# Delta-rule layer of a decoder trunk: decays on ScalarE, lengths summed on TensorE, masks later, block transfers issued by ScalarE

## The chip, the core and the metric

The kernel runs on one core of a Trainium2 chip. The metric is device time in microseconds (us) of one execution; lower is better. TensorE (PE in the rows, PEld for its weight loads), VectorE (DVE), ScalarE (ACT), GpSimd (POOL) and SyncE (SP) run their own instruction streams in order and wait for each other through semaphores. Transfers (DMAs) are started by an instruction in one of these streams; before the change that stream is SyncE's.

## The reference

A trunk of four layers on 256 positions of width 1024. Layer i mixes tokens by attention (layers 0 and 3), a short convolution (layer 1) or a gated delta rule (layer 2); each layer then has a convolutional feed-forward part (FFN). Only the delta-rule layer, `gdn` in the kernel, is changed:

```python
def gated_deltanet(h, w_in, conv_w, a_log, dt_bias, norm_w, w_o):
    ...
    q = l2norm(q) * (dh ** -0.5)          # 8 heads of 128
    k = l2norm(k)
    beta = jax.nn.sigmoid(b_logit)
    g = -jnp.exp(a_log.astype(f32)) * jax.nn.softplus(a_in + dt_bias.astype(f32))
    ...
    gc = jnp.cumsum(g, axis=-1)
    diff = gc[..., :, None] - gc[..., None, :]
    decay = jnp.where(incl, jnp.exp(jnp.where(incl, diff, 0.0)), 0.0)
    a_mat = jnp.where(strict, jnp.einsum('bhnid,bhnjd->bhnij', k_beta, k) * decay, 0.0)
    t_mat = lax.linalg.triangular_solve(a_mat + eye, ...)   # (a_mat + I)^-1
    u = t_mat @ v_beta
    attn = jnp.where(incl, jnp.einsum('bhnid,bhnjd->bhnij', q, k) * decay, 0.0)
    ...
```

The remaining lines carry a state from chunk to chunk, normalise, gate by `silu(z)` and project back.

## The kernel before, in words

**Products.** All weights come as one stream of 128 x 1024 chunks (`wraw`), loaded by SyncE. ScalarE rounds each chunk to `whi`, VectorE forms the rest `wlo`, several chunks ahead of TensorE. A product adds three matmuls per weight tile, into PSUM banks named `mm`; small matmuls go to four rotating banks named `sm`.

**Order.** TensorE's order is fixed when the program is written. `Weave` keeps a clock: the stream of products (`fill`) advances it, and generator steps such as `lengths`, `systems`, `invert` and `join_half` are put between products when they fall due; a step yields its TensorE time and how long to wait until its next one (the `L_` constants and `LAG`). The other engines' order is made by a scheduler from the data dependences. `after(inst)` binds an instruction to a place behind TensorE's last one, for that scheduler alone.

**The delta rule.** The eight heads form two halves of four, with two chunks of 128 positions, so a half has eight 128 x 128 systems. `decays` forms the decay matrices (`big`), `queries_keys` convolves q and k (`yqk`), `lengths` transposes them and sums their squares, and `systems` forms both score matrices of each system in `aq`: index 1 for keys, index 0 for queries. `invert` inverts the 16 x 16 diagonal blocks: `aq` goes to DRAM (`d<-aq`), comes back with blocks on partitions (`bl<-d`), GpSimd inverts them in 29 small steps (`xb`, `xm`), and the result goes out (`d<-xb`) and back (`xc<-d`). `join16`, `join_half(32)` and `join_half(64)` join blocks into 128 x 128 inverses, in turns between TensorE and the engines that read its results. Then come `solve`, the state, `scores` and `finish` for both chunks, and `output`, which writes `yh`, `yl` (also named `big`). The closing `residual` product consumes them: its first half of contraction (96 matmuls) needs the first half of the heads, named `o0`, its second half needs `o1`.

In `join_half` TensorE makes three groups of small matmuls (`sm<-xt,m`, `sm<-m,xt`, `sm<-xt,m`). The third is released by the copy `big<-sm` on ScalarE that empties the first group's bank:

```python
                    for m in range(NS):
                        PE.matmul(cols(pzt[up], m), lhsT=pm[dn, m, :], rhs=xt(dn, m), start=True, stop=True)
                    S.copy(s.xt[up, :, dn], wide(pzt[up, :NS * n]))
```

Of the kernel before, what the change touches and what calls it, by code (L numbers as in the profile page):

```python
# [15 lines left out]
P = 128  # L16
# [4 lines left out]
H = 8  # L21
# [17 lines left out]
SCALED = 5  # L39
LAG = 1.75  # L40
L_HEAD, L_SOFTMAX, L_TURN, L_MIX, L_READY = 3.5, 9.0, 1.0, 2.5, 0.5
L_QK, L_V, L_LEN, L_SYS, L_BLOCKS, L_JOIN, L_XI, L_PM, L_OUT = 6.0, 6.0, 1.0, 0.5, 6.0, 13.0, 1.0, 2.5, 1.0


PV_MIX = 0
# [10 lines left out]
C_ONE = C_ID + P  # L56
C_BASE = C_ONE + P
C_TRI = C_BASE + 3 * P
C_NEG = C_TRI + P
C_BD = C_NEG + P  # L60
C_LV = C_BD + P
C_UP = C_LV + P
C_EO = C_UP + P
# [4 lines left out]
def constants():  # L68
    i = np.arange(P)
    c = np.zeros((P, C_N), np.float32)  # L70
    c[:, C_ID:C_ID + P] = np.eye(P)
    c[:, C_ONE:C_ONE + P] = 1.0
    dist0 = i[:, None] - i[None, :]
    dist1 = P + i[:, None] - np.arange(2 * P)[None, :]
    base = np.concatenate([dist0, dist1], 1).astype(np.float32)
    c[:, C_BASE:C_BASE + 3 * P] = np.where(base >= 0, base, 1e33)
    c[:, C_TRI:C_TRI + P] = i[:, None] <= i[None, :]
    c[:, C_NEG:C_NEG + P] = np.where(i[None, :] >= i[:, None], 0.0, -1e30)
# [140 lines left out]
def trunk(ctx: ExitStack, tc: tile.TileContext, xT, wstream, pvec, cst, wba, hv, out):  # L219
# [380 lines left out]
    def gdn(gain):  # L600
        nm = Norm()
        NS = 2 * G_H
        with tc.tile_pool(name="gdn", bufs=1) as pool, \
# [12 lines left out]
            dl = pool.tile([P, H], F32, name="dl")  # L616
            eg = pool.tile([P, H], F32, name="eg")
            neg = pool.tile([P, H], F32, name="neg")
            yh, yl = {}, {}

            def big(dt=F32):
# [5 lines left out]
            def gates():  # L627
# [15 lines left out]
                for t in range(2):  # L643
# [19 lines left out]
                PE.matmul(pg[:, 2 * H:3 * H], lhsT=ones, rhs=g[:, 0, :], start=False, stop=True,  # L663
                          skip_group_check=True)
                V.tensor_copy(gc.rearrange("p a b -> p (a b)"), pg[:, :3 * H])
                V.tensor_sub(dl, gc[:, 2, :], gc[:, 0, :])
                S.activation(dl, dl, AF.Exp)
                S.activation(eg, gc[:, 1, :], AF.Exp)
# [6 lines left out]
            class Half:  # L675


                def __init__(self, h0):
                    self.h0, self.y = h0, []

            def decays(s):

                s.dt = big().rearrange("p (a t) i -> p a t i", t=2)
                for a2 in range(0, G_H, 2):
                    pd = bank("sm")
                    for q in range(4):
                        h, t = s.h0 + a2 + q // 2, q % 2
                        PE.matmul(pd[:, q * P:(q + 1) * P], lhsT=g[:, t, h:h + 1].to_broadcast([P, P]),
                                  rhs=tri, start=True, stop=True)
                    for q in range(4):  # L690
                        a, t = a2 + q // 2, q % 2
                        V.scalar_tensor_tensor(s.dt[:, a, t, :], pd[:, q * P:(q + 1) * P],  # L692
                                               gc[:, t, s.h0 + a:s.h0 + a + 1], cs[:, C_NEG:C_NEG + P],
                                               op0=ALU.subtract, op1=ALU.add)
                    yield 0.9, 0
                S.activation(s.dt, s.dt, AF.Exp)
                wv.set(f"d{s.h0}")

            def queries_keys(h, ps):
                yield 0, ("norm",)  # L700
                u = pool.tile([P, 2, T], F32, name="u", bufs=4)
                V.tensor_mul(u, pairs(ps), nm.rb2)
                y = pool.tile([P, 2, T], F32, name="yqk", bufs=H)
# [4 lines left out]
                halves[h // G_H].y.append(y)  # L708
                wv.set(f"q{h}", L_QK)

            def lengths(s):
# [6 lines left out]
                for a in range(G_H):  # L718
                    yield 0, (f"q{s.h0 + a}",)
                    pt = bank("sm")  # L720
                    for i in range(4):
                        q, t = divmod(i, 2)
                        PE.transpose(pt[:, i * P:(i + 1) * P], s.y[a][:, q, t * P:(t + 1) * P], ident)
                    S.copy(s.kt[:, a, :], pt[:, 2 * P:3 * P])
                    for i in range(4):
                        q, t = divmod(i, 2)
                        m = 2 * a + t
                        jk = pool.tile([P, P], F32, name="jk", bufs=1)
                        S.activation(jk, pt[:, i * P:(i + 1) * P], AF.Square, accum_out=sm[:, q, m:m + 1])  # L729
                    yield 0.22, L_LEN  # L730
                yield 0, ("gates",)

                V.tensor_scalar(sj[:, 0, :], sm[:, 0, :], EPS, float(P), op0=ALU.add, op1=ALU.mult)
# [8 lines left out]
                V.tensor_mul(s.kt, s.kt, sw.unsqueeze(2).to_broadcast([P, G_H, P]))  # L742
                wv.set(f"l{s.h0}")

            def systems(s):
# [3 lines left out]
                for a in range(G_H):  # L749
# [6 lines left out]
                    for t in range(2):  # L756
# [2 lines left out]
                            "p (q i) -> p q i", q=2), s.sk[:, m:m + 1],  # L759
                            s.dt[:, a, t, :].unsqueeze(1).to_broadcast([P, 2, P]), op0=ALU.mult, op1=ALU.mult)  # L760
                    yield 0.87, 0.5 * LAG

                nb = P // BLK
                row = (BLK * P + BLK) * nb
                d1 = dram.tile([NS * row], F32, name="d1")
                nc.sync.dma_start(
                    out=d1.rearrange("(m x) -> m x", m=NS)[:, :P * P].rearrange("m (p c) -> p m c", p=P),
                    in_=s.aq[:, :, 1, :])
                s.d1 = d1

                s.am = big()
                V.tensor_mul(s.am, s.aq[:, :, 1, :],
                             cs[:, C_UP:C_UP + P].unsqueeze(1).to_broadcast([P, NS, P]))

            def invert(s):

# [1 line left out]

                bl = pool.tile([NS * nb, BLK, BLK], F32, name="bl", bufs=1)
                with nc.allow_non_contiguous_dma(reason="16 values of a block's row"):  # L780
                    nc.sync.dma_start(
                        out=bl, in_=d1.rearrange("(q y) -> q y", q=NS * nb)[:, :BLK * P]
                        .rearrange("q (j c) -> q j c", j=BLK)[:, :, :BLK])
                xb = pool.tile([NS * nb, BLK, BLK], F32, name="xb", bufs=1)
# [8 lines left out]
                                 bl[:, k:k + 1, k + 1:].to_broadcast([NS * nb, n, r]))  # L793
                    G.tensor_sub(xb[:, :n, k + 1:], xb[:, :n, k + 1:], xm[:, :n, :r])  # L794
                d2 = dram.tile([NS, nb, BLK, BLK], F32, name="d2")
                nc.sync.dma_start(out=d2.rearrange("m b j i -> (m b) j i"), in_=xb)
                xc = pool.tile([P, NS, BLK], F32, name="xc", bufs=1)
                with nc.allow_non_contiguous_dma(reason="16 values of a block's row"):
                    nc.sync.dma_start(out=xc, in_=d2.rearrange("m b j i -> (b j) m i"))
# [141 lines left out]
            def half(s):  # L941
# [195 lines left out]
```

## Time and profile before

| | us |
|---|---|
| three timed runs | 1246.97, 1247.69, 1249.37 (median 1247.69) |
| profiled execution, its own time | 1247.2 |
| its span, first to last instruction | 1245.1 |
| TensorE busy in the span | 1225.7 (98%) |
| VectorE, ScalarE, GpSimd busy | 982.9, 775.5, 104.4 |
| delta-rule layer, its first small and its last large matmul | 585 and 756 |

The span is 2.1 us shorter than the execution's own time; that part lies around it. TensorE's granted clock is 2.4 GHz but for a few stretches at 1.2 GHz (mean 0.994 of full speed). Busy shares are means over the span; what a change in this layer can move is read from TensorE's idle stretches between these two.

### The profile page before, as it was taken

Reading aid. Unit: us, or ns where it says so; the run is one execution under the profiler, and the core shown is the slowest. Engines: PE = TensorE matmul, PEld = TensorE weight load, DVE = VectorE, ACT = ScalarE, POOL = GpSimd, SP = SyncE. Lnnn points to the kernel's source line nnn. Section 1 sums busy time; section 2 is a strip of 40 time slices with the busy share of each in tenths; the row PEclk is TensorE's granted clock in tenths of the full one; section 3 lists DMA queues with packets and bytes.
Section 4 is the critical chain, followed back from the end, with each engine's and each line's share of the span. In section 5 each row is a group of like instructions: output and inputs, shape, how many; then the busy total and the mean of one; then the engine's idle time right before and its main releaser. Section 6 shows DMA issues by size and latency. Waiting matters only on the chain.

```text
span 1245.1 us, 22068 instructions
## 1 busy us (share of the span) xinstructions
PE 1225.7 (98%) x8366; PEld 1127.5 (91%) x8366; DVE 982.9 (79%) x1720; ACT 775.5 (62%) x1427; POOL 104.4 (8%) x147
## 2 busy tenths in 40 slices
PE   9999999999999999999997999999999999999997
PEld 8989988889999988889997999988889989988886
DVE  6756999966878999866995668999775756999952
ACT  6655777644445777645873666777554655777641
POOL 2002000001002000001045102000011002000000
PEclk9999999999999999999998999999999999999998
DMA  8544465655555465655344244555655444466650
GB/s 289 200 153 166 146 201 186 213 188 189 176 182 186 153 201 193 200 189 183 126 131 126 90 136 137 200 192 189 208 190 175 156 161 165 145 202 188 211 177 34
DMA packets 67418, 215.80 MB, mean 173 GB/s; under 512 B 11248, under 2 KB 14832, under 8 KB 67312
## 3 DMA queue, kind: packets, MB, share of 16 engines
q1 hardware_dynamic: 67024, 213.86, 52.3%
q8 instruction: 66, 1.08, 0.3%
q10 hardware_dynamic: 288, 0.52, 0.1%
q14 instruction: 40, 0.33, 0.1%
HBM read 212.13 MB, written 2.23 MB: 172 GB/s over the span
## 4 chain that ended last, share of the span: by engine, by line
PE 89%; DVE 4%; ACT 2%; DMA 2%; issue 1%; POOL 1%; SPq 0%; POOLq 0%; DVEq 0%; ACTq 0%
PE mm L254 72%; PE sm L254 16%; DVE wlo L153 2%; DMA wraw<-wstream 1%; PE sm L257 1%; DVE xl L292 1%; ACT whi L152 1%; DVE yqk L422 1%; POOL xb L794 1%; POOL xm L792 1%; ACT jk L729 0%; DMA bl<-d 0%; DVE x L392 0%; DVE big L692 0%; DMA xc<-d 0%
## 5 line engine op out<-in xcount | busy, mean ns | idle before, releaser
L153 DVE TENSOR_TENSOR wlo<-wraw,whi 128x1024 fp32r<-128x1024 f32 (+1 forms) x404 | 489.5, 1212 | 155.7 <-ACT whi L152 154.0
L152 ACT CAST whi<-wraw 128x1024 fp32r<-128x1024 f32 (+1 forms) x404 | 420.2, 1041 | 290.9 <-PE mm L254 239.5
L254 PE MATMUL mm<-xh,whi 128*128 128x256 f32 x1024 | 296.5, 290 | 0.2 <-ACT whi L152 0.2
L254 PE MATMUL mm<-xh,wlo 128*128 128x256 f32 x1024 | 289.1, 282 | 1.2 <-DVE wlo L153 1.2
L254 PE MATMUL mm<-xl,whi 128*128 128x256 f32 x1024 | 288.7, 282 | 0.7 <-DVE xl L292 0.7
L254 PE MATMUL mm<-xs,whi 128*128 128x512 f32 x704 | 248.3, 394 | 0.0
L254 PE MATMUL mm<-aw,whi 128*128 128x512 f32 x704 | 247.3, 393 | 0.0
L254 PE MATMUL mm<-aw,wlo 128*128 128x256 f32 x704 | 199.1, 283 | 0.0
L254 PE MATMUL mm<-xs,wlo 128*128 128x256 f32 x704 | 199.1, 283 | 0.0
L254 PEld LDWEIGHTS mm<-xh,wlo 128*128 128x128 f32 x1024 | 193.5, 189 | 2.3 <-DVE wlo L153 2.1
L254 PEld LDWEIGHTS mm<-xl,whi 128*128 128x128 f32 x1024 | 193.8, 189 | 1.8 <-DVE xl L292 1.1
L254 PEld LDWEIGHTS mm<-xh,whi 128*128 128x128 f32 x1024 | 193.7, 189 | 1.4 <-ACT whi L152 0.4
L254 PEld LDWEIGHTS mm<-aw,whi 128*128 128x128 f32 x704 | 132.2, 188 | 30.6
L254 PEld LDWEIGHTS mm<-xs,whi 128*128 128x128 f32 x704 | 132.2, 188 | 30.5
L422 DVE SCALAR_TENSOR_TENSOR y<-u,pv,y 128x255 f32<-128x255 f32 (+1 forms) x352 | 149.0, 478 | 0.4
L254 PE MATMUL sm<-xs,whi 128*128 128x512 f32 x384 | 135.7, 393 | 0.0
L306 POOL TENSOR_TENSOR sq<-sq 128x256 f32<-128x256 f32 x62 | 53.3, 859 | 974.6 <-ACT sq L304 972.8
L254 PEld LDWEIGHTS mm<-xs,wlo 128*128 128x128 f32 x704 | 132.4, 188 | 0.0
L254 PEld LDWEIGHTS mm<-aw,wlo 128*128 128x128 f32 x704 | 132.3, 188 | 0.0
L254 PE MATMUL sm<-xs,wlo 128*128 128x256 f32 x384 | 108.6, 283 | 0.0
L420 ACT ACTIVATE y<-u,pv 128x256 f32<-128x256 f32 x176 | 81.4, 504 | 11.9 <-DVE u L451 6.6
L254 PEld LDWEIGHTS sm<-xs,whi 128*128 128x128 f32 x384 | 72.1, 188 | 16.6
(210 smaller groups left out, 1509.5 us busy)
## 6 DMA issues: line engine op xcount, KB each, us to landing
wraw<-wstream SPq DMA_DIRECT2D x396, 512.0 KB, 3.4
wraw<-wstream SPq DMA_DIRECT2D x8, 256.0 KB, 4.8
x<-xT SPq DMA_DIRECT2D x8, 128.0 KB, 4.7
d<-aq SPq DMA_DIRECT2D x2, 512.0 KB, 3.7
out<-xg ACTq DMA_DIRECT2D x2, 256.0 KB, 2.5
cs<-cst SPq DMA_DIRECT2D x1, 329.0 KB, 6.4
pv<-pvec SPq DMA_DIRECT2D x1, 324.5 KB, 4.9
cs<-cst SPq DMA_DIRECT2D x1, 320.0 KB, 5.9
```

What stands on the lines that cost most here:

```text
L152: self.nc.scalar.copy(hi[:, s], raw[:, s])
L153: self.nc.vector.tensor_sub(lo[:, s], raw[:, s], hi[:, s].bitcast(F32))
L254: self.last = nc.tensor.matmul(*a, **k)
L257: self.last = nc.tensor.transpose(*a, **k)
L292: V.scalar_tensor_tensor(xl[n], xn, col(gain + n), xh[n].bitcast(F32), op0=ALU.mult, op1=ALU.subtract)
L306: G.tensor_add(sums[0], sums[0], sq)
L420: S.activation(y, u, AF.Copy, scale=col(taps[0]))
L422: V.scalar_tensor_tensor(y[:, d:], u[:, :T - d], col(c), y[:, d:], op0=ALU.mult, op1=ALU.add)
L792: G.tensor_mul(xm[:, :n, :r], xb[:, :n, k:k + 1].to_broadcast([NS * nb, n, r]), bl[:, k:k + 1, k + 1:].to_broadcast([NS * nb, n, r]))
L794: G.tensor_sub(xb[:, :n, k + 1:], xb[:, :n, k + 1:], xm[:, :n, :r])
```

## The change

1. `decays`: ScalarE forms |c_i - c_j| from PSUM (16 instructions with `AF.Abs` and a bias from the new tile `ngc`), where VectorE had subtracted and masked. `AF.Exp` then has `scale=-1.0`. The mask is applied later, to index 0 of `aq`, by one VectorE product in each half after `join16`; the product `kt * sw` moves there as well.
2. `lengths`: ScalarE squares q and k in one instruction for each head (`sq`, in buffers named `m`), and TensorE sums the squares with four matmuls against a column of ones. Three of four transposes are dropped, and so are four squaring instructions for each head that summed as they went.
3. The four block transfers of each half are issued by ScalarE, three of them bound to places by `after`. The product `am` moves into `invert`.
4. The waits: from the last system to the join before, `L_BLOCKS` 6 and `L_JOIN` 13; now 1 + 5 + 9 + 1.5 + 1 + 4.5. `L_QK` goes from 6 to 7.5, `L_XI` from 1 to 2.

```diff
-L_QK, L_V, L_LEN, L_SYS, L_BLOCKS, L_JOIN, L_XI, L_PM, L_OUT = 6.0, 6.0, 1.0, 0.5, 6.0, 13.0, 1.0, 2.5, 1.0
+L_QK, L_V, L_LEN, L_SYS, L_XI, L_PM, L_OUT = 7.5, 6.0, 1.0, 0.5, 2.0, 2.5, 1.0
+L_STORE, L_BLOCKS, L_ROWS, L_BACK, L_MASK, L_JOIN = 1.0, 5.0, 9.0, 1.5, 1.0, 4.5
...
+                V.tensor_scalar(ngc, gc[:, :2], -1.0, None, op0=ALU.mult)
...
-                        V.scalar_tensor_tensor(s.dt[:, a, t, :], pd[:, q * P:(q + 1) * P],
-                                               gc[:, t, s.h0 + a:s.h0 + a + 1], cs[:, C_NEG:C_NEG + P],
-                                               op0=ALU.subtract, op1=ALU.add)
+                        S.activation(s.dt[:, a, t, :], pd[:, q * P:(q + 1) * P], AF.Abs,
+                                     bias=ngc[:, t, s.h0 + a:s.h0 + a + 1])
...
-                S.activation(s.dt, s.dt, AF.Exp)
+                S.activation(s.dt, s.dt, AF.Exp, scale=-1.0)
...
+                sq = pool.tile([P, 2, T], F32, name="m4", bufs=6)
+                S.activation(sq, y, AF.Square)
...
+                    PE.transpose(pt[:, :P], s.y[a][:, 1, :P], ident)
                     for i in range(4):
                         q, t = divmod(i, 2)
-                        PE.transpose(pt[:, i * P:(i + 1) * P], s.y[a][:, q, t * P:(t + 1) * P], ident)
-                    S.copy(s.kt[:, a, :], pt[:, 2 * P:3 * P])
...
-                        S.activation(jk, pt[:, i * P:(i + 1) * P], AF.Square, accum_out=sm[:, q, m:m + 1])
-                    yield 0.22, L_LEN
+                        PE.matmul(pt[:, P + i:P + i + 1], lhsT=s.sq[a][:, q, t * P:(t + 1) * P], rhs=ones[:, 0:1],
+                                  start=True, stop=True)
+                    S.copy(s.kt[:, a, :], pt[:, :P])
+                    S.copy(sm[:, :, 2 * a:2 * a + 2], pt[:, P:P + 4].rearrange("p (q t) -> p q t", q=2))
+                    yield 0.4, L_LEN
...
-                nc.sync.dma_start(
+                after(nc.scalar.dma_start(
...
-                nc.sync.dma_start(out=d2.rearrange("m b j i -> (m b) j i"), in_=xb)
+
+                yield 0, L_ROWS
+                after(nc.scalar.dma_start(out=d2.rearrange("m b j i -> (m b) j i"), in_=xb))
+                yield 0, L_BACK
...
+                    after(nc.scalar.dma_start(out=xc, in_=d2.rearrange("m b j i -> (b j) m i")))
+                yield 0, L_MASK
...
+                after(V.tensor_mul(s.kt, s.kt, s.sw.unsqueeze(2).to_broadcast([P, G_H, P])))
+
+                after(V.tensor_mul(s.aq[:, :, 0, :], s.aq[:, :, 0, :], tri.unsqueeze(1).to_broadcast([P, NS, P])))
```

Lines of the changed kernel stand one to twelve higher. Three places show what moves.

TensorE, the second of the eight steps of `lengths`, between two products (`mm`); before:

```order
L254 MATMUL mm<-xl,whi 128x256
L254 MATMUL mm<-xh,wlo 128x256
L257 MATMUL sm<-cs,yqk 128x128 x4
L254 MATMUL mm<-xh,whi 128x256
L254 MATMUL mm<-xl,whi 128x256
```

and now:

```order
L255 MATMUL mm<-xl,whi 128x256
L255 MATMUL mm<-xh,wlo 128x256
L258 MATMUL sm<-cs,yqk 128x128
L255 MATMUL sm<-cs,m_6914 128x1 x4
L255 MATMUL mm<-xh,whi 128x256
```

Four transposes (`cs` is the identity) become one transpose and four matmuls with one column (`cs` is the ones).

ScalarE, `join_half(32)` of the half that comes first; `m` is its product on the way, `xi` and `big` the copies that empty the PSUM banks; before:

```order
L860 ACTIVATE m_7742<-sm 32x256 x2
L152 CAST whi<-wraw 128x1024
L885 ACTIVATE u<-u 128x512
L871 COPY xi<-sm 32x8x32
L866 COPY big<-sm 32x8x32 x2
L895 ACTIVATE big<-sm,rn 128x128 x4
```

and now:

```order
L869 ACTIVATE m_7859<-sm 32x256 x2
L904 ACTIVATE big<-sm,rn 128x128 x4
L799 DMA d_7737<-xb 64x256
L421 ACTIVATE u<-u,pv 128x256 x2
L875 COPY big<-sm 32x8x32
L880 COPY xi<-sm 32x8x32
L803 DMA xc<-d_7737 128x8x16
L875 COPY big<-sm 32x8x32
```

Between the product `m` and the copies now stands the transfer of GpSimd's result `xb` of the other half, and behind the second copy the transfer back.

TensorE, the end of the layer: the last `scores` (`sm<-m,aq`), the last transposes of `finish` (`sm<-cs,m`), and the closing residual product (`mm<-big`), in which rows of `whi x2` and `wlo` alternate; before:

```order
L254 MATMUL mm<-xh,wlo 128x256
L254 MATMUL sm<-m_8393,aq 128x128 x4
L254 MATMUL mm<-big,whi 128x256 x2
L254 MATMUL mm<-big,wlo 128x256
...
L257 MATMUL sm<-cs,m_8462 128x128 x4
L254 MATMUL mm<-big,whi 128x256 x2
```

and now:

```order
L255 MATMUL mm<-big,wlo 128x256
L255 MATMUL sm<-m_8448,aq 128x128 x4
L255 MATMUL mm<-big,whi 128x256 x2
L255 MATMUL mm<-big,wlo 128x256
...
L258 MATMUL sm<-cs,m_8521 128x128 x4
L255 MATMUL mm<-big,whi 128x256 x2
```

Between scores and transposes stand 54 residual matmuls before and 30 now. Before, the residual product began right behind these scores, so 42 matmuls of its first half follow the transposes; now it began 66 matmuls earlier, so its first half ends at the transposes and the second half, which needs `o1`, is next. Likewise the product's start moves: it now comes 6 matmuls and one `solve` behind the transposes from which `o0` is made, and before it came 78 matmuls and all that stands between behind them.

## Rows read from the trace of the kernel before

**Rows 1.** The page: span, and busy time of each engine.

```profile
span 1245.1 us, 22068 instructions
PE 1225.7 (98%) x8366; PEld 1127.5 (91%) x8366; DVE 982.9 (79%) x1720; ACT 775.5 (62%) x1427; POOL 104.4 (8%) x147
```

**Rows 2.** Waits of TensorE, 570 to 770 us: total, times, longest.

```profile
PE sm L254 <- DVE xi L809: 5.7, 2, 5.1
PE sm L257 <- ACT yqk L707: 1.0, 1, 1.0
PE sm L254 <- ACT big L866: 0.8, 1, 0.8
...
PE sm L257 <- ACT jk L729: 0.3, 1, 0.3
```

**Rows 3.** Windows: length, busy of PE, PEld, DVE, ACT, POOL, PEclk, DMA, GB/s.

```profile
660.00:670.00 10.00, 5.82 (x27) 5.86 (x28) 5.07 (x7) 1.04 (x1) 3.65 (x4) 0.69 0.82 266
670.00:680.00 10.00, 9.42 (x124) 9.07 (x123) 7.09 (x13) 5.00 (x9) 6.78 (x17) 0.97 0.43 114
```

**Rows 4.** Timeline of TensorE around small matmuls: start, length, instruction.

```profile
615.10 0.60 PE L257 MATMUL sm<-cs,yqk 128*128 128x128 f32 x4
615.45 0.36 PE L254 MATMUL mm<-xh,whi 128*128 128x256 f32 x1
...
671.85 1.86 PE L254 MATMUL sm<-xt,big 128*128 128x16 f32 x16
...
762.87 0.50 PE L254 MATMUL sm<-cs,sq 128*128 128x1 f32 x4
763.23 0.36 PE L254 MATMUL mm<-xh,whi 128*128 128x256 f32 x1
```

**Rows 5.** Timeline, all engines: the first half's blocks, their inversion and the join.

```profile
634.68 0.38 SPq L766 DMA_DIRECT2D d<-aq  x1
637.63 0.69 SPq L781 DMA_DIRECT2D bl<-d  x1
642.39 0.49 POOL L789 TENSOR_SCALAR xb<-bl 64x15 f32<-64x15 f32 x1 [10.83 <-DMA bl<-d]
658.05 0.49 SPq L796 DMA_DIRECT2D d<-xb  x1
660.02 0.38 SPq L799 DMA_DIRECT2D xc<-d  x1
662.28 1.04 ACT L152 CAST whi<-wraw 128x1024 fp32r<-128x1024 f32 x1 [6.10 <-DMA wraw<-wstream]
664.18 3.57 PE L254 MATMUL sm<-xi,big 128*128 128x16 f32 x16 [5.09 <-DVE xi L809]
```

**Rows 6.** Timeline, all engines: last scores, last transposes, last output.

```profile
731.91 1.05 PE L254 MATMUL sm<-m,aq 128*128 128x128 f32 x8
737.47 0.69 DVE L931 TENSOR_TENSOR m<-m,f 128x512 f32<-128x512 f32 x1
739.11 0.60 PE L257 MATMUL sm<-cs,m 128*128 128x128 f32 x4
739.74 0.59 ACT L936 COPY big<-sm 128x512 f32<-128x512 f32 x1 [0.20 <-PE sm L257]
740.72 1.41 DVE L1008 SCALAR_TENSOR_TENSOR z<-big,pv,z 128x512 f32<-128x512 f32 x2
742.15 0.69 DVE L416 TENSOR_TENSOR big<-z,big 128x512 fp32r<-128x512 f32 x1
```

**Rows 7.** The chain that ended last, in order of time: start, length, what.

```profile
632.88 0.88 PE sm L254 x4
...
732.96 6.31 PE mm L254 x54
```

**Rows 8.** Windows at the kernel's end (columns of Rows 3).

```profile
1237.00:1240.00 3.00, 1.22 (x4) 0.93 (x4) 0.90 (x3) 0.00 (x0) 0.71 (x1) 0.53 0.00 0
```

**Rows 9.** The page's groups: the convolution steps on VectorE, busy and mean of one.

```profile
L422 DVE SCALAR_TENSOR_TENSOR y<-u,pv,y 128x255 f32<-128x255 f32 (+1 forms) x352 | 149.0, 478 | 0.4
```

More of the change, by code (lines that the diff above doesn't have):

```diff
@@ L58 @@
 C_TRI = C_BASE + 3 * P
-C_NEG = C_TRI + P
-C_BD = C_NEG + P
+C_BD = C_TRI + P
 C_LV = C_BD + P
@@ L77, in constants @@
     c[:, C_TRI:C_TRI + P] = i[:, None] <= i[None, :]
-    c[:, C_NEG:C_NEG + P] = np.where(i[None, :] >= i[:, None], 0.0, -1e30)
     c[:, C_ST:C_ST + 2 * H] = i[:, None] % (2 * H) == np.arange(2 * H)[None, :]
@@ L618, in gdn @@
             neg = pool.tile([P, H], F32, name="neg")
+            ngc = pool.tile([P, 2, H], F32, name="ngc")
             yh, yl = {}, {}
@@ L678, in __init__ @@
                 def __init__(self, h0):
-                    self.h0, self.y = h0, []
+                    self.h0, self.y, self.sq = h0, [], []
             def decays(s):
@@ L708, in queries_keys @@
                 halves[h // G_H].y.append(y)
+                sq = pool.tile([P, 2, T], F32, name="m4", bufs=6)
+                S.activation(sq, y, AF.Square)
+                halves[h // G_H].sq.append(sq)
                 wv.set(f"q{h}", L_QK)
@@ L720, in lengths @@
                     pt = bank("sm")
+                    PE.transpose(pt[:, :P], s.y[a][:, 1, :P], ident)
                     for i in range(4):
                         q, t = divmod(i, 2)
-                        PE.transpose(pt[:, i * P:(i + 1) * P], s.y[a][:, q, t * P:(t + 1) * P], ident)
-                    S.copy(s.kt[:, a, :], pt[:, 2 * P:3 * P])
[L725 to L728, printed above, removed]
-                        S.activation(jk, pt[:, i * P:(i + 1) * P], AF.Square, accum_out=sm[:, q, m:m + 1])
-                    yield 0.22, L_LEN
+                        PE.matmul(pt[:, P + i:P + i + 1], lhsT=s.sq[a][:, q, t * P:(t + 1) * P], rhs=ones[:, 0:1],
[3 more added lines that the diff above has]
+                    yield 0.4, L_LEN
                 yield 0, ("gates",)
@@ L741, in lengths @@
                 V.tensor_mul(sw, sk[:, 0, :], dl[:, s.h0:s.h0 + G_H])
-                V.tensor_mul(s.kt, s.kt, sw.unsqueeze(2).to_broadcast([P, G_H, P]))
+                s.sw = sw
                 wv.set(f"l{s.h0}")
@@ L761, in systems @@
                     yield 0.87, 0.5 * LAG
+                yield 0, L_STORE
                 nb = P // BLK
@@ L765, in systems @@
                 d1 = dram.tile([NS * row], F32, name="d1")
-                nc.sync.dma_start(
+                after(nc.scalar.dma_start(
                     out=d1.rearrange("(m x) -> m x", m=NS)[:, :P * P].rearrange("m (p c) -> p m c", p=P),
-                    in_=s.aq[:, :, 1, :])
+                    in_=s.aq[:, :, 1, :]))
                 s.d1 = d1
-                s.am = big()
-                V.tensor_mul(s.am, s.aq[:, :, 1, :],
-                             cs[:, C_UP:C_UP + P].unsqueeze(1).to_broadcast([P, NS, P]))
             def invert(s):
@@ L780, in invert @@
                 with nc.allow_non_contiguous_dma(reason="16 values of a block's row"):
-                    nc.sync.dma_start(
+                    nc.scalar.dma_start(
                         out=bl, in_=d1.rearrange("(q y) -> q y", q=NS * nb)[:, :BLK * P]
@@ L795, in invert @@
                 d2 = dram.tile([NS, nb, BLK, BLK], F32, name="d2")
-                nc.sync.dma_start(out=d2.rearrange("m b j i -> (m b) j i"), in_=xb)
+                yield 0, L_ROWS
+                after(nc.scalar.dma_start(out=d2.rearrange("m b j i -> (m b) j i"), in_=xb))
+                yield 0, L_BACK
                 xc = pool.tile([P, NS, BLK], F32, name="xc", bufs=1)
                 with nc.allow_non_contiguous_dma(reason="16 values of a block's row"):
-                    nc.sync.dma_start(out=xc, in_=d2.rearrange("m b j i -> (b j) m i"))
+                    after(nc.scalar.dma_start(out=xc, in_=d2.rearrange("m b j i -> (b j) m i")))
+                yield 0, L_MASK
+                s.am = big()
+                after(V.tensor_mul(s.am, s.aq[:, :, 1, :],
+                                   cs[:, C_UP:C_UP + P].unsqueeze(1).to_broadcast([P, NS, P])))
                 s.xt32 = pool.tile([P, NS, 2, BLK], F32, name="xt32", bufs=2)
```

## The prediction

> **What bounds the kernel now.** First the page: TensorE is busy 1225.7 of 1245.1 us [rows 1], so time can be won or lost only where it idles, where its clock is low, and in the work it is given. Then its waits in the layer that is changed: 5.7 + 1.0 + 0.8 + 0.3 = 7.8 us [rows 2], of which 5.1 us is one stall before the first join. Then the granted clock by windows: 0.69 in 660 to 670 us and 0.97 in the next ten [rows 3]. With levels of 1 and 0.5 that is (3.1 + 0.3) / 0.5 = 6.8 us at 1.2 GHz; TensorE idled 5.1 us before 664.18 and the low stretch then lasted to about 670.6. Of it 6.4 us fell on work, which lost 3.2 us. So at most 7.8 + 3.2 = **11.0 us** are to be had, three quarters of them at that join.
>
> The timeline there shows the cause [rows 5]: `aq` leaves at 634.68, blocks start back at 637.63, GpSimd inverts from 642.39 to 658.05, the result goes out and starts back at 660.02, TensorE resumes at 664.18. That chain is 29.5 us long, and SyncE stands still in it: a weight chunk's rounding waits 6.10 us for its transfer.
>
> **The change part by part.** All 54 products in 6.31 us [rows 7] give 0.117 us for one large matmul; distances in TensorE's new order are counted with it.
>
> *Lengths.* Four transposes take 0.35 us to the next matmul's start [rows 4]. Matmuls of one column in fp32 run as two passes each: the two of a norm show as four passes, 0.36 us [rows 4]. A step has now one transpose (0.09) and eight passes (0.72): 0.81, so 0.46 more than before, and there are eight steps: **+3.7 us** of TensorE work. From above, sixteen passes of 16 columns take 1.86 us, 0.116 each [rows 4]: 8 x (0.09 + 0.93 - 0.35) = 5.4. From below I allow a fifth off: 3.0. I take 3.7, the row of the same form.
>
> A page speaks against this part more sharply. The Trainium skill, "TensorE: Matmul & The Clock Gate", section "LDWEIGHTS (loading the stationary operand)", says that a weight load costs its number of columns over 1.2 ns, however little is multiplied with it. By that a pass costs an estimated 0.107 us, and these eight steps an estimated 4.9 us in place of 3.7, which would make the sum below 1256.4. The row of one column shows 0.09, so the page's figure is not used.
>
> *Decays.* Sixteen instructions go from VectorE to ScalarE, which in turn makes eight squares in place of 32. None of it is TensorE time, and TensorE's products of the next heads cover it. But decays, squares and two `Exp` now stand ahead of the fourth head's `Silu`, so I leave 0.3 of the old 1.3 us of waits for lengths [rows 2].
>
> *First join.* In the new order TensorE reaches it 234 large matmuls (27.4 us) and 5.7 us of small ones (two steps of lengths, 0.9 each with the gap behind them, four of systems at 0.88 [rows 7], transposes 0.44) behind the first half's last system: 33.1 us. The chain of 29.5 us starts 1.0 us behind that system and grows: on ScalarE `d<-aq` stands behind a convolution that waits for VectorE (+1.5), `bl<-d` behind two weight roundings and a `Silu` (+0.3), and on VectorE the transpose `xi` now stands behind six convolution steps (149.0 / 352 = 0.42 each [rows 9], +2.4). That is 34.7, 1.6 us more than TensorE's way, and 1.9 with the 0.3 above. The six steps may end sooner if their data is early; I take **1.5 us for both**, between 0 and 4 (without the six steps, or with two roundings more).
>
> *Second half's inversion.* ScalarE executes its stream in order, so `d<-xb` holds what is behind it until GpSimd is done. Count from the start X of the first join. `xc` of the first half was issued at X - 6.4 (3.1 to land, 0.45 for `xt`, 2.4, 0.45 for `xi`; without the 2.4 it was 4.16 from 660.02 to 664.18 [rows 5]). Behind it on ScalarE: two roundings (1.9), the second half's `d<-aq`, and its blocks back 2.95 us later (634.68 to 637.63), at X - 1.5. GpSimd starts 4.76 us after that and needs 15.7 [rows 5], or 14 if it is a little luckier: done at X + 17.3 to 18.9. ScalarE then does two convolutions and `big<-sm`, 1.2 us, and only this copy releases the third group of `join_half(32)`. TensorE is there at X + 14.0: 1.7 for the join's own, 6 matmuls, transposes 0.44, 18 matmuls, again 1.7 (1.86 with its tail [rows 4]), 24 matmuls, 1.0, transposes 0.44, 18 matmuls, and two groups of 0.5. It idles 4.5 to 6 us where it had 0.8 [rows 2]. I take **4.5 us**, since any slack at the first join shortens it; 0 if GpSimd is faster (below), 6 from above.
>
> The Trainium skill, "DMA: Bandwidth & Descriptors", section "Anatomy of one DMA", says that a transfer's semaphore wait happens on the issuing sequencer before dispatch. This trace agrees for SyncE, in the 6.10 us of rows 5; the change hands the same waiting to an engine that computes.
>
> *The end.* Three covers go, by the order shown above. (a) Last scores to last transposes: before, scores end at 732.96 and VectorE's `m` that is transposed at 738.16 [rows 6], 5.2 us covered by 54 matmuls (6.31). Now 30 matmuls cover 3.5: 1.7 us idle. (b) Last transposes (end 739.71) to `yl`, which the second matmul of the residual's second half reads: first `yl` done at 742.84 [rows 6], 3.1 us, less the 0.4 between the copy's end and `z`, in which VectorE was at a weight: 2.7 us, then covered by 42 matmuls (4.9), now by none: 2.7 us idle. (c) The same path for `o0`, 3.3 us with a gate product between: 6 matmuls and a `solve` cover 1.6, so 1.7 us idle. Together **6.1 us**, none of it there before; 5 if the copies run without a neighbour, 8 with one more `wlo` and one rounding in the way.
>
> *Clock.* TensorE fell to 1.2 GHz after the stall of 5.1 us [rows 2, 3], and also at the kernel's end, 0.53 in 1237 to 1240 [rows 8], where short idles alternate with little work. The new idles at the join and the end resemble these. I count one such loss of **3.2 us**; none to two, 0 to 6.4.
>
> *Priced at nothing.* SyncE is free for weights, but TensorE's waits in rows 2 name no weight. The mask and `kt` products (VectorE, 79% busy [rows 1]) fall in the joins, where `scores` is over ten steps away; with that cover gone they would cost about 1.9 us once. `am` only moves.
>
> **Sum**, against the profiled execution's 1247.2: + 3.7 lengths + 1.5 to the first join + 4.5 at `join_half` + 6.1 at the end + 3.2 clock - 11.0 = + 8.0, so 1255.2. The runs' median is 0.5 above that execution; I say **1255**. All bounds low: 3.0 + 0 + 0 + 5.0 + 0 - 11.0 = - 3.0 (1244). All high: 5.4 + 4 + 6 + 8 + 6.4 - 11.0 = + 18.8 (1266).
>
> **The rivals.**
> *A, the other side: ScalarE is never held.* GpSimd's 15.7 us [rows 5] are 29 steps, 0.54 us on average, where the first takes 0.49; the time of a step may hang on what VectorE does beside it, and VectorE's work is now placed otherwise. At 0.38 us a step the inversion takes 11 us, and both `d<-xb` find it nearly done. It decides from 12 us down. Then the join and the first stall are gone: 3.7 + 0.3 + 0 + 6.1 - 11.0 = - 0.9, 1246.3, and with a clock loss at the end 1249.5. For it: VectorE makes no more decays. Against it: those lie ahead of the inversion, and within it VectorE keeps its weights and gets two products more for each half. The end's idles stay in any case. 27 in 100.
> *B, the change doesn't do what it says: the first join waits as before.* If `d<-aq` and `bl<-d` each find ScalarE busy with one rounding more, about 1 us each, and the inversion starts 3 to 4 us later, the old stall of 5.1 with its 3.2 is back in place of 1.5: about 1262. For it: everything that leaves ScalarE here is queued; against it: TensorE's own longer way of 33.1 us. 9 in 100.
> *C, the lengths are hidden.* If one-column passes run under the wide matmul ahead of them, + 3.7 becomes 0: 1251.5 with the rest as forecast, 1243 together with A. Rows 4 speak against it: the four passes push the next matmul back by their full 0.36. 4 in 100.
>
> **Chances and range.** The forecast, 60 in 100, gives 1250 to 1262 by its bounds. About 0.2%, 2.5 us, is what a measurement of this kernel tells from no change, so 1245.2 to 1250.2 is the same. Faster: the lower third of A and half of C's, 12 in 100. Same: the rest of A and the forecast's lowest edge, 20. Slower: 68. A range of 1246 to 1263 leaves out the lowest of A and C and the highest of B and the forecast, 2 in 10.
>
> **What would show it.** Right, step by step: in TensorE's timeline a step of `lengths` 0.8 us long; in its waits some 4 us for `big` of `join_half` and, ahead of it on ScalarE, idle time put down to `xb` or its transfer; idles of 1.7, 1.7 and 2.7 us for ScalarE's and VectorE's output path around the residual product; the granted clock at 0.5 in one stretch of the layer. Wrong: an inversion of 11 us on GpSimd, no wait for `big`, or a clock of 1.00 through to the FFN.

## The result, and the profile after

The changed kernel takes **1259.8 us** (median of 4 runs), the kernel before in the same session 1248.2: ratio 1.0099, 95% interval 1.0071 to 1.0126. That is slower, by about 12 us, inside the range and 5 us above the forecast. The profiled execution took 1259.5 us; its page begins

```profile
span 1257.7 us, 22105 instructions
PE 1234.3 (98%) x8406; PEld 1135.6 (90%) x8406; DVE 981.2 (78%) x1707; ACT 773.0 (61%) x1395; POOL 104.5 (8%) x147
```

The span is 12.6 us longer than in [rows 1], and TensorE's busy time grew by 8.6 of these: work, or a slower clock. The waits of TensorE in the layer, 570 to 790 us (what it waited for, us, times, longest), answer to [rows 2]:

```profile
PE mm L255 <- ACT big L416: 2.8, 2, 2.1
PE sm L255 <- ACT big L875: 2.7, 1, 2.7
PE sm L255 <- DVE xi L818: 2.4, 1, 2.4
PE sm L258 <- DVE m L940: 2.4, 1, 2.4
PE sm L255 <- ACT m L916: 1.3, 1, 1.3
PE mm L255 <- DVE big L417: 0.7, 1, 0.7
...
```

The row left out, 0.2 us, comes behind the layer. One stall of 5.1 us and four of 1.0 and less have become seven of 0.6 to 2.7; their sum went from 7.8 to 12.3 us. The windows of the same layer (columns of [rows 3]) where the granted clock is below 1.00:

```profile
670.00:680.00 10.00, 9.09 (x66) 9.12 (x67) 8.02 (x15) 5.17 (x10) 6.25 (x18) 0.83 0.45 132
690.00:700.00 10.00, 10.00 (x94) 9.56 (x94) 6.23 (x10) 6.05 (x12) 0.00 (x0) 0.83 0.23 61
710.00:720.00 10.00, 8.62 (x123) 8.10 (x122) 7.03 (x13) 5.37 (x12) 1.03 (x1) 0.89 0.17 54
720.00:730.00 10.00, 10.00 (x93) 9.56 (x91) 3.65 (x7) 5.98 (x14) 1.01 (x1) 0.94 0.08 18
750.00:760.00 10.00, 6.05 (x31) 5.36 (x31) 4.80 (x8) 2.28 (x5) 0.71 (x1) 0.66 0.26 97
```

(1.7 + 1.7 + 1.1 + 0.6 + 3.4) / 0.5 = 17.0 us at 1.2 GHz, where before had 6.8. By windows of 1 us, some 14.4 of them fall on work: a loss of 7.2 us, in four places, each in or behind one of the stalls (2.4 us, 2.7 us, 1.3 us, and the pair of 2.4 and 2.1 at the end). Before lost 3.2 in one.

A step of lengths in TensorE's timeline (start, length, what), against the first of [rows 4]:

```profile
615.33 0.27 PE L258 MATMUL sm<-cs,yqk 128*128 128x128 f32 x1
615.44 0.95 PE L255 MATMUL sm<-cs,m 128*128 128x1 f32 x8
616.25 0.36 PE L255 MATMUL mm<-xh,whi 128*128 128x256 f32 x1
```

From the step's start to the next product's it is 0.92 us, where it was 0.35: 8 x 0.57 = 4.6 us. So the longer span is made of 4.5 us of waits, 4.0 of clock and 4.6 of work, 13.1 for 12.6 measured.

The stall at `join_half(32)`, timeline of all engines:

```profile
687.88 0.24 POOL L795 TENSOR_TENSOR xb<-xb,xm 64x15 f32<-64x15 f32 x1
688.15 0.47 ACTq L799 DMA_DIRECT2D d<-xb  x1
688.66 0.91 ACT L421 ACTIVATE u<-u,pv 128x256 f32<-128x256 f32 x2 [2.63 <-POOL xb L795]
689.48 0.35 ACT L875 COPY big<-sm 32x256 f32<-32x256 f32 x1
689.88 0.69 PE L255 MATMUL sm<-xt,m 32*32 32x32 f32 x16 [2.72 <-ACT big L875]
```

Read it upwards: TensorE waits 2.72 us for a copy of 0.35; ScalarE stood idle 2.63 us ahead of it, not for want of data but because the next thing in its order was the transfer of `xb`, which GpSimd finished at 688.12. The Trainium skill, "DMA: Bandwidth & Descriptors", section "Anatomy of one DMA — SWDGE (gpsimd) path", puts a transfer's semaphore wait on the issuing sequencer. This row, of a transfer issued by ScalarE, agrees, and gives the price where that sequencer also has copies to make.

The first join, where TensorE waits 2.44 us for `xi`; ScalarE's row, then VectorE's:

```profile
661.75 2.02 ACT L153 CAST whi<-wraw 128x1024 fp32r<-128x1024 f32 x2 [2.22 <-DMA d<-xb]
664.76 1.22 DVE L807 TENSOR_TENSOR big<-aq,cs 128x1024 f32<-128x1024 f32 x1
666.49 1.22 DVE L154 TENSOR_TENSOR wlo<-wraw,whi 128x1024 fp32r<-128x1024 f32 x1
667.63 0.42 DVE L811 TENSOR_TENSOR xt<-xc,cs 128x256 f32<-128x256 f32 x1
667.96 2.44 DVE L423 SCALAR_TENSOR_TENSOR u<-u,pv 128x255 f32<-128x255 f32 x6
670.33 0.43 DVE L818 STREAM_TRANSPOSE xi<-xt 128x256 f32<-128x256 f32 x1
```

The result `xb` left at 657.84 and ScalarE idled 2.22 us until it had landed, 3.40 us later; in [rows 5] the way back starts 1.97 us after the way out. `xc` left at 661.26 and landed 2.1 us later. VectorE, busy from 662.83 on, came to it at 667.63, behind the product `am` (L807, moved here by the change) and the rest of a weight, among others; then come six convolution steps ahead of `xi`.

The two waits at the layer's end:

```profile
750.95 0.69 DVE L940 TENSOR_TENSOR m<-m,f 128x512 f32<-128x512 f32 x1
751.69 0.93 PE L258 MATMUL sm<-cs,m 128*128 128x128 f32 x4 [2.39 <-DVE m L940]
753.28 1.41 DVE L1020 SCALAR_TENSOR_TENSOR z<-big,pv,z 128x512 f32<-128x512 f32 x2 [0.51 <-ACT big L945]
754.74 1.31 PE L255 MATMUL mm<-big,whi 128*128 128x256 f32 x2 [2.11 <-ACT big L416]
```

TensorE ran out of residual products twice in 6 us and worked on at half speed until 758.6.

### The profile page after: what moved, and what is told of

Read it like the earlier page. It is cut to its first block, busy times and chain, and to the rows that moved or that the text cites. A ratio compares the mean times of both kernels' runs of the same rounds, so it can differ in the third digit from the quotient of the medians.

```text
span 1257.7 us, 22105 instructions
## 1 busy us (share of the span) xinstructions
PE 1234.3 (98%) x8406; PEld 1135.6 (90%) x8406; DVE 981.2 (78%) x1707; ACT 773.0 (61%) x1395; POOL 104.5 (8%) x147
## 3 DMA queue, kind: packets, MB, share of 16 engines
q10 hardware_dynamic: 6688, 1.97, 0.6%
## 4 chain that ended last, share of the span: by engine, by line
PE 90%; DVE 3%; POOL 2%; DMA 2%; issue 2%; ACT 1%; SPq 0%; ACTq 0%; POOLq 0%; DVEq 0%
PE mm L255 73%; PE sm L255 16%; POOL xb L795 1%; POOL xm L793 1%; DVE wlo L154 1%; PE sm L258 1%; DVE xl L293 1%; DMA d<-aq 1%; DMA bl<-d 0%; DMA x<-xT 0%; ACT whi L153 0%; DVE x L393 0%; DMA d<-xb 0%; DVE z L1020 0%; DVE xg L1062 0%
```

## The experiments

The kernel before took 1248.7 us beside runs 1 to 4, 1247.9 beside 5 to 8, 1248.8 beside 9 to 11 and 1248.9 beside 12. Waits and windows are those of the layer, 570 to 800 us.

**1. All transfers on SyncE.** In the changed kernel, four times:

```
-                after(nc.scalar.dma_start(
+                after(nc.sync.dma_start(
```

> The changed kernel, with the four transfers of the blocks issued by SyncE again; where they stand in the order, the lags and all else stay. My theory (ScalarE, held by the result's transfer until GpSimd is done, delays the copy that TensorE waits for in join_half(32)): the wait of 2.7 us there goes, and the 1.6 us that the low clock behind it took, so 1254 to 1257, if no weight comes late because SyncE now stands still. Rival (the engine that issues doesn't matter, the longer lags at the end and the lengths cost it all): 1259 to 1261, with a wait of about 2.7 us still there.

Measured 1256.8 us, ratio to before 1.0063 (1.0050 to 1.0076): 3.0 below the changed kernel, in time as expected. No wait is left for the copy; the first join's, for `xi`, shrank from 2.4 to 0.9, a wait of 1.3 for `Silu` came in, and the clock is low for 17.0 us as in the changed kernel.

**2. Only the way back on SyncE.** The same for `d<-xb` and `xc<-d` alone.

> The changed kernel, with only the way back of the blocks (the result out, and the blocks of 16 in again) issued by SyncE; the way there stays on ScalarE. My theory: this pair alone holds ScalarE, so the same 1254 to 1257 and no wait of over 1 us for the copy in join_half(32). Rival (it is the way there, queued behind ScalarE's work, that makes the inversion late): 1259 to 1260, the wait for the first join's xi as long as now, 2.4 us, and the one in join_half too.

1254.6 us, ratio 1.0049 (1.0036 to 1.0061): 5.3 us won, half of the loss, by moving four instructions to another queue. Its waits:

```profile
PE mm L255 <- ACT big L416: 2.8, 2, 2.1
PE sm L258 <- DVE m L940: 2.4, 1, 2.4
PE sm L255 <- ACT m L916: 1.3, 1, 1.3
PE sm L255 <- DVE xi L818: 0.8, 1, 0.8
PE mm L255 <- DVE big L417: 0.7, 1, 0.7
```

The end's waits are untouched. The copy's wait is gone and so is that at the first half's first join: the 0.8 us for `xi` left in the list stand at 695.61, at the second half's. The clock is low for 13.6 us in place of 17.0. ScalarE held by the way back is shown as a cause, at both joins.

**3. Lengths by transposes again.** The eight squares behind `Silu` go too.

```
-                        PE.matmul(pt[:, P + i:P + i + 1], lhsT=s.sq[a][...], rhs=ones[:, 0:1], ...)
-                    S.copy(s.kt[:, a, :], pt[:, :P])
+                        PE.transpose(pt[:, i * P:(i + 1) * P], s.y[a][...], ident)
+                    S.copy(s.kt[:, a, :], pt[:, 2 * P:3 * P])
+                        S.activation(jk, pt[:, i * P:(i + 1) * P], AF.Square, accum_out=...)
```

> The changed kernel, with lengths as before: four transposes a step, and ScalarE squares with sums; no squares behind Silu. My theory (eight passes of one column cost TensorE 0.46 us more a step than three transposes): 3.7 us less, 1255 to 1257. Rival (they run in gaps that TensorE has anyway): 1259 to 1261, or more where ScalarE's 24 further instructions make its transfers later.

1262.1 us, ratio 1.0115 (1.0100 to 1.0130): not the 3.7 us faster that was expected; whether it is slower than the changed kernel is not told, since the intervals overlap. TensorE has 4.6 us less work and waits longer:

```profile
PE mm L255 <- ACT big L416: 4.4, 2, 2.3
PE sm L255 <- ACT whi L153: 3.4, 1, 3.4
...
PE sm L255 <- ACT jk L732: 1.6, 2, 0.9
```

The 3.4 us stand at the first join, where `xi` is ready at 669.91 and `whi`, which the list names, at 669.98. With decays on ScalarE too, its 32 squares make lengths late (`jk`), the transfers behind them leave 1.9 us later (`d<-aq` at 638.36 for 636.46), and the clock is low for 23.8 us, not 17.0. The passes do cost TensorE what they take; the transposes are no cheaper in their place while ScalarE has the rest.

**4. Lags as short as before.**

```
-L_QK, ..., L_XI, ... = 7.5, ..., 2.0, ...
-L_STORE, L_BLOCKS, L_ROWS, L_BACK, L_MASK, L_JOIN = 1.0, 5.0, 9.0, 1.5, 1.0, 4.5
+L_QK, ..., L_XI, ... = 6.0, ..., 1.0, ...
+L_STORE, L_BLOCKS, L_ROWS, L_BACK, L_MASK, L_JOIN = 0.0, 5.0, 9.0, 1.5, 1.0, 2.5
```

> The changed kernel, with the planned times as short as before (6.0 for queries and keys, 19.0 from the stored system to the join, 1.0 for xi). My theory (the longer way to the join takes the cover from the three waits at the layer's end, 1.3 + 2.4 + 2.1 us and some 4 us of low clock behind them): these waits shrink by about 5 us and some of the clock's loss goes, but the first join waits 5 to 7 us in place of 2.4 since the chain is as long as it was: 1254 to 1258 in all. Rival (the lags cost nothing, since what is late in the end is late by the same amount as in the join): 1259 to 1262.

1256.3 us, ratio 1.0064 (1.0048 to 1.0079). As expected in time; the end's waits shrank from 5.8 to 0.6 us. The first join did not wait 5 to 7 but 1.3, since TensorE came late itself: it had waited 1.8 us for lengths and 2.7 for `Silu`. The clock's loss did not shrink: it is low for 17.0 us as in the changed kernel, now ahead of the end.

**5. The stall filled, in the kernel before.**

```
                 pp = bank("sm")
+                for _ in range(0 if s.h0 else 40):
+                    PE.matmul(pp[:, :T], lhsT=xh[0][:, :P], rhs=xh[0], start=True, stop=True)
```

> The kernel before with one addition: in the stall of 5.1 us ahead of the first half's first join, TensorE executes 40 products of 128 by 256 of the layer's input whose result is overwritten (4.7 us at 0.117 each). Nothing else is changed, nothing is computed sooner. My theory on the clock (a stall of a few us makes TensorE fall to 1.2 GHz, and that fall costs 3.2 us of work): the granted clock stays at 1.00 through 660 to 680 us and the kernel is 3.2 us faster, 1244 to 1246. Rival (the low clock there comes from something else, or these products don't count as work): the clock falls as before and the time is 1247 to 1250.

1248.2 us, ratio 0.9999 (0.9987 to 1.0012): the time of the rival, though the clock did not fall where the rival had it fall. TensorE's timeline at the two first joins, and the windows:

```profile
658.11 4.95 PE L254 MATMUL sm<-xh 128*128 128x256 f32 x40
663.21 1.96 PE L254 MATMUL sm<-xi,big 128*128 128x16 f32 x16 [0.15 <-DVE xi L809]
691.95 3.57 PE L254 MATMUL sm<-xi,big 128*128 128x16 f32 x16 [3.29 <-DVE xi L809]
```

```profile
660.00:670.00 10.00, 9.85 (x85) 9.64 (x84) 7.19 (x10) 2.90 (x4) 2.73 (x2) 1.00 0.86 280
670.00:680.00 10.00, 9.96 (x148) 9.36 (x146) 6.45 (x12) 6.83 (x15) 6.83 (x16) 1.00 0.23 63
690.00:700.00 10.00, 8.05 (x38) 8.08 (x39) 5.89 (x11) 2.31 (x7) 0.00 (x0) 0.54 0.51 163
```

The clock stayed at 2.4 GHz through the first join, and the products there take 1.96 us in place of the 3.57 of [rows 5]. But TensorE then came to the second half's first join at 688.66, where it had started it at 693.82, and `xi` was only ready at 691.95; it waited 3.3 us and worked 9.1 us at 1.2 GHz, a loss of 4.6. In this execution what was won at one join was given back at the next. But it is the longest of twelve, 1249.7 us at a mean clock of 0.993; nine others have 0.995 and a median of 1248.1, no faster than before either. So the second fall of the clock is not the whole reason.

**6. Copies behind both starts.** In `join_half` of the changed kernel:

```
                     for m in range(NS):
                         PE.matmul(cols(pzt[up], m), lhsT=pm[dn, m, :], rhs=xt(dn, m), start=True, stop=True)
+                for b in starts:
+                    up, dn = slice(b, b + n), slice(b + n, b + 2 * n)
                     S.copy(s.xt[up, :, dn], wide(pzt[up, :NS * n]))
```

> The changed kernel; in join_half the copies out of the bank come behind the matmuls of both starts, not between them, so that no group of TensorE waits in the middle for ScalarE's copy. My theory (TensorE needs nothing of that copy but its place in the bank; ScalarE, held by the blocks' transfer, is only in the way there): the wait of 2.7 us for the copy goes, with the 1.6 us of the low clock behind it; 1254.5 to 1257, like issuing the way back from SyncE (1254.6). Rival (what ScalarE does late is needed soon after in any case): the wait comes back at a later group with nearly its length, and the time is 1258 to 1261.

1261.4 us, ratio 1.0099 (1.0078 to 1.0120), the rival's time. The wait for the copy is gone, and ScalarE is held all the same, now for the blocks in DRAM:

```profile
692.33 1.05 ACT L153 CAST whi<-wraw 128x1024 fp32r<-128x1024 f32 x1 [1.56 <-DMA d<-xb]
694.70 0.66 PE L258 MATMUL sm<-cs,u 128*128 128x128 f32 x4 [1.70 <-ACT u L896]
```

TensorE waits 1.7 us for the `Silu` behind it, and 2.1 in place of 1.3 for `m`: 2.5 us for the 2.7 that went. Beside that, the same stall of 2.4 us at the first join is followed by 6.8 us at 1.2 GHz in this execution, by 3.4 in the changed kernel's. The copy itself waits for the engine that is held, so sparing TensorE the copy only moved the wait.

**7. Decays alone, in the kernel before.**

```
-                        V.scalar_tensor_tensor(s.dt[:, a, t, :], pd[...], gc[...], cs[:, C_NEG:C_NEG + P], ...)
+                        S.activation(s.dt[:, a, t, :], pd[...], AF.Abs, bias=ngc[...])
```

> The kernel before with the first part of the change alone: the decays as Abs with a bias on ScalarE, and the mask of the scores behind the first join. Lengths, transfers and lags are those of before. My theory (the parts that cost are the lengths' passes, the held ScalarE and the lags): within 2 us of before, 1247 to 1250; if anything the waits for lengths, now queued behind the decays, grow from 1.3 to about 2.5 us. Rival (VectorE's relief is worth something on the way to the first join, since its inversion runs slow beside VectorE): the stall of 5.1 us shrinks, 1243 to 1246.

1250.5 us, ratio 1.0022 (1.0008 to 1.0035): slightly slower. Waits for lengths went from 1.3 to 2.3 us (all for `jk` now), the stall from 5.1 to 4.0, there is one more fall of the clock, 0.83 in 680 to 690 us, and a wait of 1.0 for `m` of the solve came in.

**8. The findings combined**: runs 2 and 6 in one, with lags between the two.

```
+L_QK, ..., L_XI, ... = 7.0, ..., 1.0, ...
+L_STORE, L_BLOCKS, L_ROWS, L_BACK, L_MASK, L_JOIN = 1.0, 5.0, 8.0, 1.5, 1.0, 3.0
```

> The changed kernel with what the runs so far point to: the way back of the blocks on SyncE, the copies of join_half behind both starts, and lags between the two (7.0 for queries and keys, 18.5 from the stored system to the join, 1.0 for xi). My theory: no wait at join_half, most of the end's cover back (waits of about 1 us of 6.4), 1 to 3 us at the first join, one or two falls of the clock: 1247 to 1252. Rival (TensorE's waits only change their place, since the chain from lengths to the end is too long for the fill): 1254 to 1257.

1255.3 us, ratio 1.0060 (1.0038 to 1.0081): the rival, and not told from run 2. The eight executions go from 1253.3 to 1261.4, and the profiled one is the longest, so its trace need not hold for the others. `xi` is waited for twice in it, 3.6 and 3.1 us. ScalarE's timeline shows why the second half is late there:

```profile
664.18 0.41 ACTq L771 DMA_DIRECT2D d<-aq  x1
...
675.71 1.05 ACT L153 CAST whi<-wraw 128x1024 fp32r<-128x1024 f32 x1 [5.73 <-PE mm L255]
675.79 0.59 ACTq L782 DMA_DIRECT2D bl<-d  x1
```

The blocks start back 11.6 us after they left, behind a rounding that waits 5.73 us for TensorE to be through with a weight; TensorE had itself stalled for the first join until 668.61. So the way there can be held on ScalarE too, by work that has nothing to do with it.

**9. The second join later, with the stall filled**: run 5, run 6's order of copies, and

```
-                yield 0, L_JOIN
+                yield 0, L_JOIN + (2.5 if s.h0 else 0.0)
```

> The kernel with the filled stall, in which the second half's first join is planned 2.5 us later (15.5 for 13.0, the first half's stays) and join_half copies behind both starts. With the stall filled, TensorE came to the second half's first join 5.2 us sooner than before and waited 3.3 us there for xi, with a fall of the clock behind it; that took back all that the filling had won. My theory (the second half's chain of transfers and inversion does not come sooner when TensorE does, so time won at the first join has to be covered with other work at the second): the wait there is under 1 us, the clock stays up, the end keeps its cover: 1242 to 1245. Rival (the 2.5 us are missing at the end instead): the same 1247 to 1250, with waits of 2 us and more around the residual product.

1253.0 us, ratio 1.0034 (1.0021 to 1.0046): slower than the kernel before and than run 5, outside both expectations. The join was put later and waited 3.5 us all the same, now at 696.22. VectorE's timeline:

```profile
691.79 0.43 DVE L802 TENSOR_TENSOR xt<-xc,cs 128x256 f32<-128x256 f32 x1 [1.53 <-DMA xc<-d]
692.13 1.22 DVE L153 TENSOR_TENSOR wlo<-wraw,whi 128x1024 fp32r<-128x1024 f32 x1
693.27 2.45 DVE L422 SCALAR_TENSOR_TENSOR u<-u,pv 128x255 f32<-128x255 f32 x6
695.63 0.44 DVE L809 STREAM_TRANSPOSE xi<-xt 128x256 f32<-128x256 f32 x1
```

The transpose `xi` stands behind a weight and six steps of a convolution: 3.4 us between `xt`'s end and `xi`. Nor did the clock stay up: at the first join, behind the same 40 products and a wait of 0.5 us, it fell at 665.5 for 3.4 us. Two things were changed beside run 5, so what each of them cost is open.

**10. Longer lags alone, in the kernel before.**

```
-L_QK, ..., L_BLOCKS, L_JOIN, L_XI, ... = 6.0, ..., 6.0, 13.0, 1.0, ...
+L_QK, ..., L_BLOCKS, L_JOIN, L_XI, ... = 7.5, ..., 6.0, 16.0, 2.0, ...
```

> The kernel before with only lags as long as those of the change (7.5 for queries and keys, 6.0 + 16.0 to the join, 2.0 for xi). My theory (longer lags take the stall from the first join and give it to the end): the stall of 5.1 us and its 3.2 us of low clock go, some 5 us of waits come at the end with a fall of the clock there: 1246 to 1250. Rival A (the lags are what makes the change slow): 1252 or more. Rival B (the stall was the whole loss): 1240 to 1244.

1250.1 us, ratio 1.0012 (1.0003 to 1.0021). The time is my theory's, the trace only half:

```profile
PE sm L254 <- DVE xi L809: 4.1, 1, 4.1
PE mm L254 <- ACT big L415: 3.2, 1, 3.2
```

The join, planned later, still waits 4.1 us, because `xi` came later too (666.92 for 664.18, though the blocks left at 634.90 for 634.68); 3.2 us came at the end. `xc` had left sooner than in [rows 5], at 658.94 for 660.02, but VectorE, busy with the rest of a weight from 662.21, two systems and a product `am`, came to `xt` only at 665.40; before, it waited for `xc` and had `xt` at 663.13. Longer lags so also put other work ahead of `xi`.

**11. Lengths alone, in the kernel before**: run 3's edit the other way round.

> The kernel before with only the lengths of the change: a square of y by ScalarE, one transpose and four products of one column a step. My theory (3.7 us more of work on TensorE; the chain to the first join is no shorter, so the work takes the place of waiting where it stands ahead of the chain, and is added where it stands in it): 1248 to 1252, with TensorE's waits for lengths gone (1.3 us) and the stall of the first join as long as before. Rival (the work is hidden in the stall, since it stands ahead of it): 1245 to 1248.

1251.5 us, ratio 1.0025 (1.0014 to 1.0036). As expected in time: the added work stands ahead of the chain, which starts 4.4 us later (`d<-aq` at 639.07), and the stall is 3.3 for 5.1. Waits for lengths did not go; they are 1.7 us, now for `yqk` and its square.

**12. Both joins filled, in the kernel before**: run 5's loop with

```
+                for _ in range(28 if s.h0 else 40):
```

> The kernel before with both first joins' waits filled: 40 products of no use ahead of the first half's, as in the run with the filled stall, and 28 (3.3 us) ahead of the second half's, where that run waited 3.3 us and then worked from 692.0 to about 701.1 us at 1.2 GHz. The plan and all else are those of before. My theory (the filling wins 3.2 us at the first half's join; what took it back is the low clock behind the wait at the second one, 9.1 us of work at half speed, so 4.6 us): the clock stays up at both, 1242.5 to 1245. Rival (the chain of the second half, not the clock, sets the end, and what TensorE does sooner it waits for later): 1247 to 1250, with the waits now at a later step.

1247.1 us, ratio to before 0.9992 (0.9982 to 1.0003): not told from it, and in the rival's range, though no long wait came back. The profiled execution took 1245.3, with the clock at 1.00 through the whole layer:

```profile
690.00:700.00 10.00, 10.00 (x90) 10.00 (x89) 7.25 (x14) 4.26 (x13) 0.00 (x0) 1.00 0.56 203
700.00:710.00 10.00, 9.66 (x137) 8.97 (x136) 5.04 (x11) 6.26 (x17) 1.03 (x1) 1.00 0.16 54
```

Against run 5's profiled execution the span is 4.4 us shorter, the 4.6 of low clock. Over all executions the gain is smaller (their mean granted clock lies between 0.994 and 0.998). Against before, what remains after both clock losses are avoided is 1 to 2 us: the second half's first join starts at 691.9 for 693.8. Its `xi` is ready at 693.0 before, 691.8 in run 5 and 691.0 here, though TensorE is at that place at 693.8, 688.7 and 688.5: coming some 5 us sooner brought the chain forward by 1.2 to 2.0. Here the filling itself holds TensorE for the last 0.9.

## Why the prediction was right, and where it was off

**Direction and range**: right, and most of the steps as put. The waits forecast in their places add up to 12.1 us (1.5 first join, 4.5 `join_half`, 6.1 end); all measured ones to 12.3. That these agree is in part luck, since one term came out larger, two smaller, and one wait had no place in the sum, as follows.

**Lengths**: the mechanism right, the term mis-sized: 4.6 us in place of 3.7. A pass of the eight takes (616.25 - 615.44) / 8 = 0.101 us, not the 0.09 of [rows 4]. The Trainium skill, "TensorE: Matmul & The Clock Gate", section "LDWEIGHTS (loading the stationary operand)", gives 0.107 for 128 columns, and the estimate of 4.9 worked out from it was nearer than my row. The 0.3 us left for waits for lengths did not come.

**First join**: 2.4 for 1.5, a size nearly right by a chain that was not. The six convolution steps ahead of `xi` are there. Not foreseen: `xb` took 3.40 us to land for 1.97, and `xt` was late by VectorE's order. It starts 6.4 us after `xc` left, where I had counted 3.1, with `am` among the work ahead of it, which I had put at nothing as it "only moves". GpSimd took back 2.7 of this: it started 3.0 us after its blocks were called, not 4.8, and needed 14.8 us, not 15.7. Why `xb` landed late is not shown by a run of its own; SyncE had sent off a weight 0.1 us ahead of it, where before the weight came behind. With the way back on SyncE there is no wait (run 2).

**`join_half`**: the held ScalarE is confirmed by run 2, at 5.3 us for both joins, waits and clock together. The wait itself was 2.7 for 4.5. I had counted GpSimd's end from X + 17.3; it came at 688.12, X + 17.2. That is luck: it started at X + 1.5, not X + 3.3, and needed 15.7 us, not the 14 behind that bound. TensorE's arrival I had put at X + 14.0; it was 687.16, X + 16.3, some 1.7 us of it since the low clock behind X (3.4 us) made its way longer, and that I had not let into this step. Beside it stands a wait of 1.3 us for `m` of the solve that I did not foresee; it is in runs 1 and 2 too and gone in run 4. Run 7 has 1.0 us of it with decays alone and the old lags, and run 10, with longer lags alone, none: so the decays' part can bring it alone. Why run 4 is free of it is open.

**The end**: 2.4, 2.1 and 0.6 + 0.7 for (a), (b), (c), against 1.7, 2.7 and 1.7; 5.8 for 6.1. Run 4, where 0.6 is left, shows that the lags are the cause.

**Clock**: this step failed by most. I counted one loss of 3.2 us because the stalls resembled the old one of 5.1. It fell four times, at stalls of 1.3 to 2.7, and that cost 7.2. With the lengths' 0.9 that is the 5 us between forecast and measurement. That a stall alone makes it fall is not shown: in run 2 it fell behind a wait of 0.8.

**The ceiling of 11.0 us** ("at most 7.8 + 3.2 are to be had") was worked out rightly and was misleading: run 12 fills the first join's stall, avoids both clock losses, and wins at most 2 us. Filled time isn't won time, of course, and no run takes the stall itself away. But runs 5 and 12 bring TensorE to the second half's first join 5 us sooner, and its `xi` comes only 1.2 to 2.0 us sooner. By these two runs I estimate that the next chain of transfers and inversion would have taken back most of what the first one gave.

**Shares.** Alone on the kernel before, decays cost 0.22%, lengths 0.25% and lags 0.12%, together 0.59 of the 0.99%. The rest, 0.40%, is left for the transfers, for the products that moved (`am`, `kt`), which no run has alone, and for what the parts do to each other; moving the way back off ScalarE returns 0.50%. Why the way there on ScalarE did well in run 2 against run 1 (1254.6 and 1256.8, intervals that overlap) stays open; the traces differ by run 1's wait of 1.3 us for `Silu` and one more fall of the clock. Rival A, an inversion of 11 us, did not come true: it took 14.8 and 15.7 us. Nor did B (the first join waits 2.4 us, not 5.1) or C (a step of lengths is 0.92 us long).

## What to carry to other kernels

A transfer that waits for a slow producer belongs on a queue whose engine has nothing else to do: four instructions on ScalarE cost nearly half of this change. Before a stall is priced as gain, look for the next place that waits for the same kind of chain, and ask whether that chain comes sooner too; here a stall ahead of a second, equally long chain was worth little. And several short stalls can cost more clock than one long one, 7.2 us for 3.2 here, so a change that spreads one over several places has to be charged for the clock at each.

## What the runs showed of the hardware

In the changed kernel TensorE fell from 2.4 to 1.2 GHz in a stall of 1.3 us (717.0 to 718.4) and stayed there for 3.4 us, as it did behind stalls of 2.4 and 2.7. In run 5 it stayed for 10.2 us at one of 3.3, in the kernel before for 6.8 at one of 5.1. The stall's length does not settle it: a wait of 0.8 us for `big` was followed by a fall in run 7 and by none before, and the first join's 2.4 us by 3.4 us of low clock in the changed kernel and by 6.8 in run 6.

Products whose result is never read kept it at 2.4 GHz in two profiled executions: 40 of them in 4.95 us at the first join (runs 5 and 12), 28 in 3.52 at the second (run 12). In run 9 it fell 2.4 us behind the end of the same 40, for 3.4 us.

A transfer of 64 KB issued by ScalarE 0.1 us behind a weight of 512 KB on SyncE's queue landed in 3.40 us; issued by SyncE with the weight behind it, it landed in 2.0 (the kernel before and run 2).
